# The attention heads' gate as seven half-size products, the residual gate's sums at an earlier place, and a new order of the projections

## The chip, the cores and the metric

The kernel runs on one core of a Trainium2 chip, as one program with one launch. The metric is the device time of that program in microseconds. The engines in the text are PE (TensorE), DVE (VectorE), ACT (ScalarE) and POOL (GpSimd). SP (SyncE) does no arithmetic here: it issues nearly all transfers between the chip's memory and the on-chip buffers, in one queue, in order.

## The reference, cut to what matters

One layer with 1,024 latent tokens (`x`), 256 context tokens and a model width of 1,024. Both token sets are normalised and modulated, then multiplied by one wide input matrix whose output is cut into eleven parts.

```
pl = project(modulate(x, sh_x, sc_x), w_in)       # gq gk gv gg lr dq dk dv dg mg md
pc = project(modulate(ctx, sh_c, sc_c), w_in)
o_gla  = bidir_gla(...)                           # gated linear attention, from gq gk gv and the decay
o_diff = diff_attention(...)                      # from dq dk dv, over context and latent keys
a = merge_heads(rms_norm(o_gla) * gla_gain) * silu(gla_gate)              # gla_gate  = pl[3] (gg)
b = merge_heads(rms_norm(o_diff) * diff_gain * (1 - lam_init)) * silu(diff_gate)   # diff_gate = pl[8] (dg)
y = sigmoid(m_gla) * (a @ w_br_gla) + sigmoid(m_diff) * (b @ w_br_diff)
x = x + g_x * (y @ w_out)                         # g_x: the last third of silu(c) @ w_ada + b_ada
```

`dg` is the part that this change computes in another way: 1,024 tokens by 1,024 columns from an inner width of 1,024. `g_x` is the residual gate.

## The kernel before

Matrix products keep near float32 precision by cutting each operand into a high and a low part, so every product of tiles is three PE instructions (`mm3`, high by high, high by low, low by high). A piece of weight comes by DMA into a `raw` buffer (three of them, 512 KB each), ACT writes the high part and DVE the low part (`split`), both into tiles called `w` (18 of them, so nine pairs).

The order of instructions on PE, ACT, DVE and POOL is not written out. Tasks (Python generators) run under a planner, `Driver`, which keeps its own estimate of every engine's clock and lets the ready task of the best priority write its next instructions. PE then runs what it was given strictly in that order. SP's order is set by another scheduler. Stages in order of time:

1. The modulated inputs `h` are made, then the projections gk, gq and gg (first half of the columns) run on PE. Beside them run the decays (`job_la`, tiles `gs`, `go`, `gt` into `g5`) and `sums`, in which DVE adds and subtracts blocks of `h` (S2, S1, S3, S4), splits them and stores them to `d_s`.
2. `pairs`: the projections gv and dv as seven half-size products (Winograd's form of Strassen's scheme). Rows, columns and inner width are halved. Five tiles of 128 rows (four of latent tokens, one of context) by four inner pieces by seven products by three instructions make 420 PE instructions for one projection; the plain way takes 10 x 8 x 2 x 3 = 480. The left operands S come back from `d_s` through six `g5` buffers (task `loads`). The right operands are sums of weight blocks that DVE makes in place and splits (`pair_weights`). Results are collected in on-chip tiles X, U, U5 with ACT copies and DVE additions (`copy`, `add`, `out`, `direct`).
3. `to_gla` closes the buffers of the pairs and opens those of the GLA; it first waits for the residual gate's store (`ev_gb`). Four GLA heads then run as chains of small PE, ACT, DVE and POOL steps. The other projections (list `late`, plain form) have the lowest priority and fill PE between those steps: dk, second half of gg, second half of dk, first half of dg, first half of dq, one block of mg, second half of dq, second half of dg. At the fourth of them (`n == 3`) `rope_tables(0)` is started, which loads and scales the table that `post_qk` of dq needs.
4. When the last head's results are written, `to_gla` opens the attention's buffers (`ev_b2`); queries `aq`, keys `hk` and values `vv` are loaded, and when the projections are done (`ev_stream`) the attention of the eight heads runs (tiles `s`, `e`, `b`, `mb`). The output product follows.

The residual gate is made by `job_gate`: eight weight pieces of 512 KB pass through the `raw` buffers, DVE multiplies and adds them into `gb` (16 instructions), PE sums over partitions with `ones`, DVE adds the bias, POOL halves it, and one store writes `d_gb`. It is started when the second pair (dv) begins, and its first line waits until all weights of the pairs are loaded (`ev_pl`).

`post_gate` turns a finished tile of gg or dg into its gate: ACT tanh, one DVE instruction, one POOL multiplication by a gain, a store.

Of the kernel before, what the change touches and what calls it, by code (L numbers as in the profile page):

```python
# [20 lines left out]
P = 128  # L21
# [207 lines left out]
class Hybrid:  # L229
# [515 lines left out]
    def job_gate(self):  # L745


        yield self.ev_pl
# [63 lines left out]
    def phase_a(self):  # L812
# [40 lines left out]
        wp = self.pair_weights((C_GV, C_DV), wd.loaded[-1], last)  # L853
# [20 lines left out]
        d.spawn(self.consts_late(), At(105.0), prio=2)  # L874
        d.spawn(self.sums(), prio=3)
# [7 lines left out]

    SUMS = ("s2", "s1", "s3", "s4")

# [32 lines left out]
    def pair_weights(self, cols, ev_load, ev_run):  # L918
# [3 lines left out]
        wp = {(g, n, k): Event() for g in range(2) for n in RIGHT for k in range(4)}  # L922
# [4 lines left out]
        ev_l = {(g, n, kk): Event() for g in range(2) for n, kk, _ in LOADS}  # L927
# [13 lines left out]
        def run():  # L941
            yield ev_run
            for g in range(2):
# [43 lines left out]
    def pairs(self, wp):  # L987
# [3 lines left out]
        def loads():  # L991

            for g in range(2):
# [4 lines left out]
            for g in range(2):  # L998
# [22 lines left out]
        def mms(g, n, k, t, pm, first, last):  # L1021
# [5 lines left out]
            if t == 4:  # L1027
# [6 lines left out]
        for g in range(2):  # L1034
            if g:
                d.spawn(self.job_gate(), prio=2)
# [4 lines left out]
            def out(g, r, c, t, x, tag):  # L1041

                o = self.tok(8 + r if t == 4 else 4 * r + t)
                if g == 0:
                    self.store([(self.d_v[c][o:o + P], x)], (tag, 1))
                    return
# [39 lines left out]
            for t in range(5):  # L1086
# [7 lines left out]
            for n, ev, dst, nxt, tag in (("p6", "x", U, "u", "x2"), ("p5", "u", U5, "u5", "p")):  # L1094
                for k in range(4):
                    for t in range(5):
# [5 lines left out]
            for t in (0, 1, -1, 2, -2, 3, -3, 4, -4, -5):  # L1102
# [9 lines left out]
            for k in range(4):  # L1112
                for t in range(5):
# [6 lines left out]
    def direct(self, g, t, pm, tag):  # L1120

        o = self.tok(8 if t == 4 else t)
        if g == 0:
# [216 lines left out]
    def post_gate(self, dif, c, i, pm):  # L1340
# [6 lines left out]
        self.rel("mm", e)  # L1347
# [1075 lines left out]
```

## Time and profile before

| | us |
|---|---|
| median of 3 runs | 1690.53 |
| lowest and highest | 1687.66, 1690.86 |
| the profiled execution | 1693.12 |
| its span, first to last instruction | 1691.4 |
| PE busy in the span | 1649.2 (98%) |
| DVE, ACT, POOL busy | 1140.7 (67%), 781.4 (46%), 617.6 (37%) |

The rows used stand in a section further down. The page gives totals and the chain of work that ended last; the stage table gives busy time per engine and stretch, the granted clock as a share of full speed, and the share of time and the rate at which the 16 DMA engines moved data; the timeline gives single instructions, with the engine's idle time before them in brackets. PE instructions overlap: the duration of one is longer than the distance from its start to the next one's, so a price per instruction is read from a merged run of many.

### The profile page before, as it was taken

The page shows a single profiled execution, that of the slowest core. Times are in us where ns is not written, and L with a number is a line of the kernel's source. Part 1 is how long each engine was busy: PE and PEld are TensorE (multiplying, and loading weights), DVE is VectorE, ACT ScalarE, POOL GpSimd, SP SyncE. Part 2 cuts the span into 40 slices and gives each one's busy share as a digit, 9 for nine tenths or more (in the row PEclk, how much of TensorE's full clock was granted, in tenths as well). Part 3 has the DMA queues.
Part 4 walks back from the last instruction along what each step waited for, and adds up shares of the span by engine and source line. Part 5 has one row for each costly group of instructions (what it writes and reads, how often), then busy time and mean ns, then how long its engine had stood idle before and what let it go on. Part 6 is the DMA issues. An engine that isn't in the chain of part 4 may idle for free.

```text
span 1691.4 us, 24621 instructions
## 1 busy us (share of the span) xinstructions
PE 1649.2 (98%) x8437; PEld 1366.0 (81%) x8437; DVE 1140.7 (67%) x2027; ACT 781.4 (46%) x1632; POOL 617.6 (37%) x743
## 2 busy tenths in 40 slices
PE   7999999999999999999999999999999899999999
PEld 3788888888888888888887788888887787887887
DVE  4787743466856866775553988777787787526694
ACT  4766522343444445455232666655656555411231
POOL 1500300002554655553342555455665455700000
PEclk9999999999999999999999999999999999999999
DMA  8556847588737466453851444436368451279431
GB/s 306 172 202 235 303 159 266 178 280 284 224 119 222 134 177 197 131 177 108 245 163 53 106 116 122 129 91 162 104 172 251 140 164 60 91 234 340 151 100 75
DMA packets 259950, 293.43 MB, mean 173 GB/s; under 512 B 21961, under 2 KB 182641, under 8 KB 259825
## 3 DMA queue, kind: packets, MB, share of 16 engines
q1 hardware_dynamic: 259824, 291.85, 55.0%
q8 instruction: 67, 1.10, 0.3%
q14 instruction: 59, 0.48, 0.1%
HBM read 194.27 MB, written 97.52 MB: 173 GB/s over the span
## 4 chain that ended last, share of the span: by engine, by line
PE 82%; DVE 7%; DMA 5%; ACT 2%; issue 2%; POOL 2%; SPq 0%; DVEq 0%; ACTq 0%; POOLq 0%
PE mm L335 33%; PE mc L335 10%; PE mb L335 7%; PE s L335 6%; PE b L335 5%; PE go L335 4%; PE b L361 3%; PE tp L335 3%; PE gt L335 3%; DVE sm L197 3%; PE gs L335 3%; PE tp L361 2%; POOL at L197 2%; DVE e L197 1%; ACT e L197 1%
## 5 line engine op out<-in xcount | busy, mean ns | idle before, releaser
L335 PE MATMUL mm<-w,h 128*128 128x512 f32 x1608 | 401.6, 400 | 0.0
L335 PEld LDWEIGHTS mm<-w,h 128*128 128x128 f32 x1608 | 297.4, 188 | 60.1 <-issue 0.5
L197 DVE TENSOR_REDUCE sm<-s 128x1 f32<-128x1024 f32 (+1 forms) x192 | 194.5, 1038 | 23.9 <-PE s L335 22.0
L335 PE MATMUL mb<-h,wt 128*128 128x512 f32 x744 | 205.1, 408 | 2.5 <-ACT ft L197 2.1
L197 ACT ACTIVATE e<-s,sm 128x1280 f32<-128x1280 f32 x128 | 170.1, 1331 | 69.2 <-DVE sm L197 61.5
L197 POOL TENSOR_TENSOR at<-ac,at 128x512 fp32r<-128x512 f32 x128 | 185.1, 1446 | 10.7
L335 PE MATMUL s<-hk,aq 128*128 128x512 f32 (+1 forms) x768 | 180.7, 369 | 4.1 <-issue 1.5
L197 POOL TENSOR_SCALAR at<-ac 128x512 fp32r<-128x512 f32 x128 | 100.7, 787 | 202.2 <-ACT ac L197 182.6
L335 PEld LDWEIGHTS mb<-h,wt 128*128 128x128 f32 x744 | 131.1, 190 | 25.9 <-ACT ft L197 3.6
L335 PEld LDWEIGHTS s<-hk,aq 128*128 128x128 f32 x768 | 124.3, 193 | 24.9 <-ACT e L197 4.9
L335 PE MATMUL mm<-h,w 128*128 128x512 f32 x576 | 142.4, 398 | 1.4 <-DVE h L197 1.0
L335 PE MATMUL mc<-h,wt 128*128 128x512 f32 x600 | 140.8, 392 | 1.4 <-DVE wt L197 0.5
L197 POOL TENSOR_TENSOR sm<-sm,nhalf 128x1 f32<-128x1 f32 (+2 forms) x110 | 113.8, 1035 | 56.4 <-DVE sm L197 49.6
L335 PEld LDWEIGHTS mc<-h,wt 128*128 128x128 f32 x600 | 111.4, 188 | 26.1 <-DMA h<-d_bT 2.4
L335 PE MATMUL b<-at,vv 128*128 128x256 f32 x960 | 131.9, 287 | 0.5 <-POOL at L197 0.4
L335 PEld LDWEIGHTS b<-at,vv 128*128 128x128 f32 x960 | 124.1, 192 | 5.7 <-POOL at L197 1.2
L335 PEld LDWEIGHTS mm<-h,w 128*128 128x128 f32 x576 | 106.1, 188 | 23.6 <-DVE h L197 1.5
L197 ACT ACTIVATE p<-mm 128x512 f32<-128x512 f32 (+1 forms) x111 | 64.1, 587 | 130.0 <-PE mm L335 112.0
L197 ACT ACTIVATE ac<-b 128x512 f32<-128x512 f32 x120 | 71.3, 601 | 89.6 <-PE b L361 84.4
L197 DVE SCALAR_TENSOR_TENSOR e<-e,sm,e 128x1280 f32<-128x1280 f32 x64 | 108.7, 1699 | 0.6
L197 DVE TENSOR_TENSOR w<-raw,w 128x512 fp32r<-128x512 f32 x120 | 88.0, 751 | 29.1 <-ACT w L197 24.2
L361 PE MATMUL b<-ident,e 128*128 128x128 f32 x598 | 93.3, 277 | 14.2 <-DVE b1k L197 4.8
(282 smaller groups left out, 2697.4 us busy)
## 6 DMA issues: line engine op xcount, KB each, us to landing
raw<-in_w_in SPq DMA_DIRECT2D x66, 512.0 KB, 4.7
g<-d_s SPq DMA_DIRECT2D x32, 640.0 KB, 5.3
aq<-d_qT SPq DMA_DIRECT2D x128, 128.0 KB, 3.1
d_dv<-pl SPq DMA_DIRECT2D x40, 256.0 KB, 5.3
d_kT<-pl SPq DMA_DIRECT2D x40, 256.0 KB, 2.9
gv<-d_v SPq DMA_DIRECT2D x40, 256.0 KB, 3.2
hk<-d_kT SPq DMA_DIRECT2D x32, 320.0 KB, 5.2
vv<-d_dv SPq DMA_DIRECT2D x16, 640.0 KB, 5.9
```

The lines of the kernel that those rows point to most:

```text
L197: self.ins = f(out, *args, **kw).ins
L335: self.ins = self.nc.tensor.matmul(out, lhsT, rhs, start=start, stop=stop, skip_group_check=more).ins
L361: self.nc.tensor.transpose(out, src, self.ident[:n, :n])
```

## The change

`dg` leaves the plain projections and becomes the third member of `pairs`, after gv and dv, for the latent tokens only: four tiles of rows in place of five, `nt = 4 if what == "dg" else 5`. Its left operands are the first 512 columns of the stored S. The gate of three of its four blocks is made from the on-chip sums in `out` (tanh, one DVE instruction, one POOL multiplication), that of the last from the accumulator in `direct` by `post_gate`. `job_gate` no longer waits for `ev_pl` and is started at the planner's time 110, beside the projections gq and gg. The list `late` is now dk, dk, second half of gg, dq, dq and, put in at place 5, mg; at `n == 3`, where `rope_tables(0)` is started, stands the first half of dq.

```diff
     def job_gate(self):
-        yield self.ev_pl
...
-        dg = nat(C_DG, (x8, x8), lambda c, i, pm: self.post_gate(1, c, i, pm))
-        late = [dk[0], gg[1], dk[1], dg[0], dq[0], dq[1], dg[1]]
+        late = [dk[0], dk[1], gg[1], dq[0], dq[1]]
         NM = 1
         for m in range(NM):
             late.insert(5, tra(C_MG + m * 512, ...))
...
-        wp = self.pair_weights((C_GV, C_DV), wd.loaded[-1], last)
+        wp = self.pair_weights([c for _, c in self.BY7], wd.loaded[-1], last)
...
+        d.spawn(self.job_gate(), At(110.0), prio=2)
...
+    BY7 = (("gv", C_GV), ("dv", C_DV), ("dg", C_DG))
...
+            for g, (what, _) in enumerate(self.BY7):
+                w = 512 if what == "dg" else 640
...
-                        z = self.t("g5", [P, 2, 640], F32R)
-                        self.dma(z, self.d_s[n, k])
+                        z = self.t("g5", [P, 2, w], F32R)
+                        self.dma(z, self.d_s[n, k][:, :, :w])
...
-        for g in range(2):
-            if g:
-                d.spawn(self.job_gate(), prio=2)
+        for g, (what, _) in enumerate(self.BY7):
+            nt = 4 if what == "dg" else 5
...
+                if self.BY7[g][0] == "dg":
+                    yield from self.acq("p")
+                    th = self.t("p", [P, 512])
+                    yield d.on("ACT", x)
+                    yield On(self.act.activation(th, x, AF.Tanh, scale=0.5), "DVE")
+                    e = self.dve.scalar_tensor_tensor(x, th, 1.0, x, ALU.add, ALU.mult)
+                    self.rel("p", e)
+                    yield e
+                    xv = x.rearrange("p (n w) -> p n w", w=P)
+                    self.pool.tensor_tensor(xv, xv, self.gdif..., ALU.mult)
+                    self.store([(self.d_dg[c][...], x)], (tag, 1), ev=...)
+                    return
...
-            for t in (0, 1, -1, 2, -2, 3, -3, 4, -4, -5):
+            for t in (0, 1, -1, 2, -2, 3, -3, 4, -4, -5) if nt == 5 else (0, 1, -1, 2, -2, 3, -3, -4):
```

In the program's order this shows at three places. The first is PE at the end of dv. Before, the first tile of dk follows, eight inner pieces into one accumulator `mm`; `h` are the pieces of the modulated input.

```order
L335 MATMUL mm_3564<-w_3455,h_73_382 128x512
L335 MATMUL mm_3564<-w_3456,h_73_382 128x512
L335 MATMUL mm_3564<-w_3455,h_74_383 128x512
L335 MATMUL mm_3564<-w_3465,h_131_582 128x512
L335 MATMUL mm_3564<-w_3466,h_131_582 128x512
L335 MATMUL mm_3564<-w_3465,h_132_583 128x512
```

The same place of the changed program, where dg's products begin:

```order
L335 MATMUL mm_3596<-w_3487,h_73_382 128x512
L335 MATMUL mm_3596<-w_3488,h_73_382 128x512
L335 MATMUL mm_3596<-w_3487,h_74_383 128x512
L335 MATMUL gt_3611<-w_3518,h_131_582 128x512
L335 MATMUL gt_3611<-w_3519,h_131_582 128x512
L335 MATMUL gt_3611<-w_3518,h_132_583 128x512
```

After the fourth inner piece the accumulator changes from `mm` to `gt`: two products of half the inner width stand where one of the full width stood. Over the whole program PE has 48 rows fewer, DVE 41 more, ACT 24 more, SP 18 more and POOL as many as before.

The second place is DVE at the start of the projection gg, where the low parts of its seventh and eighth weight pieces are made. Before (`w_1720` and `w_1732` are those two; `g` and `x` belong to `sums` and to the decays):

```order
L197 TENSOR_TENSOR w_1683<-raw_1391,w_1682 128x512
L197 TENSOR_TENSOR g_314_1561<-g_314_1561,x_331_1681 128x640
L197 TENSOR_SCALAR g_336_1698<-gs_1699,col 128x512
L197 TENSOR_SCALAR g_336_1698<-go_1702,col 128x512
L197 TENSOR_SCALAR g_336_1698<-gt_1706,col 128x256
L197 TENSOR_TENSOR w_1720<-raw_1652,w_1719 128x512
L197 TENSOR_TENSOR g_314_1561<-g_314_1561,x_334_1696 128x640
L197 TENSOR_TENSOR w_1732<-raw_1652,w_1731 128x512
```

The same stretch now, where `w_1754` and `w_1762` are the two pieces:

```order
L197 TENSOR_TENSOR w_1698<-raw_1623,w_1697 128x512
L197 TENSOR_TENSOR g_318_1580<-g_318_1580,g_317_1579 128x640
L197 TENSOR_SCALAR gb_1143<-raw_1667,col 128x512
L197 TENSOR_SCALAR g_341_1710<-gs_1711,col 128x512
L197 SCALAR_TENSOR_TENSOR gb_1143<-raw_1667,col,gb_1143 128x512
L197 TENSOR_TENSOR g_317_1579<-g_317_1579,x_339_1708 128x640
L197 TENSOR_SCALAR g_341_1710<-go_1716,col 128x512
L197 TENSOR_SCALAR g_341_1710<-gt_1720,col 128x256
L197 TENSOR_TENSOR w_1754<-raw_1695,w_1753 128x512
L197 TENSOR_TENSOR g_317_1579<-g_317_1579,x_345_1728 128x640
L197 TENSOR_TENSOR w_1762<-raw_1695,w_1761 128x512
```

Two instructions of the residual gate and one more of `sums` now stand between the sixth weight piece and the seventh.

The third place is SP at the end of the GLA. `d_aT` are its last results, `aq` the attention's first queries, `d_qT` the queries of the projection dq, `vv` the attention's values. Before, with plain projections still to come:

```order
L300 DMA d_aT_99<-gpl_8261 128x2x128
L300 DMA aq_8323<-d_qT_86 64x2x256 x2
L300 DMA aq_8326<-d_qT_86 64x2x256 x2
L300 DMA aq_8329<-d_qT_86 64x2x256 x2
L300 DMA aq_8332<-d_qT_86 64x2x256 x2
L300 DMA d_qT_87<-pl_8300 128x4x128
L300 DMA d_qT_87<-pl_8301 128x4x128
L300 DMA vv_8378<-d_dv_82 128x10x128
L300 DMA vv_8380<-d_dv_84 128x10x128
```

The same place of the changed program, where `d_m` are stores of the mg block and `raw` the next weights:

```order
L300 DMA d_aT_99<-gpl_8894 128x2x128
L300 DMA d_m_117<-p_8907 128x512
L300 DMA aq_8936<-d_qT_86 64x2x256 x2
L300 DMA aq_8939<-d_qT_86 64x2x256 x2
L300 DMA aq_8942<-d_qT_86 64x2x256 x2
L300 DMA aq_8945<-d_qT_86 64x2x256 x2
L300 DMA raw_8968<-in_w_in 128x8x128
L300 DMA vv_8979<-d_dv_82 128x10x128
L300 DMA vv_8981<-d_dv_84 128x10x128
L300 DMA vv_8983<-d_dv_82 128x10x128
L300 DMA raw_8999<-in_w_in 128x8x128
L300 DMA d_m_118<-p_9001 128x512
```

One store of the mg block (`d_m`) now stands ahead of the queries, and only two such stores are left behind them: on PE 54 products of mg stand between the GLA's last instruction and the attention's first, where 351 products of dq and dg stood. From the attention's first instruction on, the order on PE (3,161 rows), DVE and ACT is the same in both programs.

## Rows read from the trace of the kernel before

**Rows 1.** The page: busy time and share of each engine, then the last chain.

```profile
PE 1649.2 (98%) x8437; PEld 1366.0 (81%) x8437; DVE 1140.7 (67%) x2027; ACT 781.4 (46%) x1632; POOL 617.6 (37%) x743
...
PE 82%; DVE 7%; DMA 5%; ACT 2%; issue 2%; POOL 2%; SPq 0%; DVEq 0%; ACTq 0%; POOLq 0%
```

**Rows 2.** Busy time by stage, from gq to the attention's start; columns in its first line.

```profile
core 0: us, PE busy (x) PEld busy (x) DVE busy (x) ACT busy (x) POOL busy (x), PEclk, DMA share, GB/s
100.00:160.00 60.00, 60.00 (x313) 51.56 (x312) 45.17 (x67) 42.42 (x61) 0.00 (x0) 1.00 0.59 212
160.00:208.80 48.80, 48.80 (x217) 40.40 (x216) 40.16 (x51) 26.79 (x39) 11.88 (x8) 1.00 0.87 318
208.80:303.60 94.80, 94.80 (x420) 78.51 (x419) 40.34 (x62) 28.48 (x49) 1.40 (x1) 1.00 0.61 217
303.60:398.40 94.80, 93.92 (x412) 77.08 (x412) 53.93 (x84) 34.53 (x60) 0.62 (x1) 1.00 0.71 245
398.40:442.00 43.60, 43.60 (x203) 35.62 (x202) 33.10 (x54) 10.51 (x19) 21.36 (x24) 1.00 0.86 268
442.00:825.50 383.50, 382.06 (x1932) 320.88 (x1931) 256.81 (x508) 185.44 (x525) 199.34 (x331) 1.00 0.56 164
825.50:910.60 85.10, 83.60 (x384) 68.77 (x383) 39.52 (x64) 20.26 (x33) 34.10 (x31) 1.00 0.50 144
```

**Rows 3.** Timeline of PE: start, length, instructions, idle before; first gg, then dv.

```profile
161.85 4.24 PE L335 MATMUL mm<-w,h 128*128 128x512 f32 x18
...
166.50 42.35 PE L335 MATMUL mm<-w,h 128*128 128x512 f32 x186
...
381.08 0.97 PE L335 MATMUL tp<-w,hk 128*128 128x512 f32 x3 [0.88 <-DVE p L197]
```

**Rows 4.** Groups by line: count, then busy us, mean ns, idle before.

```profile
L197 DVE TENSOR_TENSOR w<-l,w 128x512 fp32r<-128x512 f32 x28 | 18.7, 687 | 16.9 <-ACT w L197 16.9
...
L197 DVE SCALAR_TENSOR_TENSOR gb<-raw,col,gb 128x512 f32<-128x512 f32 x14 | 11.4, 814 | 4.9 <-DMA raw<-in_w_ada 4.8
...
L197 ACT ACTIVATE w<-l 128x512 fp32r<-128x512 f32 x28 | 17.0, 626 | 17.3 <-PE go L335 15.6 <-PE mm L335 1.5
...
L197 POOL TENSOR_TENSOR p<-p,gdif 128x512 f32<-128x512 f32 x16 | 22.0, 1379 | 35.8 <-DVE p L197 35.6 <-PE gt L361 0.2
...
L335 PE MATMUL go<-gv,gsc 128*128 128x256 f32 x64 | 19.1, 381 | 0.2 <-DVE gsc L197 0.2
```

**Rows 5.** DMA issues: count, KB each, median us to landing.

```profile
g<-d_s SPq DMA_DIRECT2D x32, 640.0 KB, 5.3
...
raw<-in_w_ada SPq DMA_DIRECT2D x12, 512.0 KB, 6.0
```

**Rows 6.** Timeline of SP and DVE: gg's last weight piece, load and split.

```profile
156.36 0.38 SPq L300 DMA_DIRECT2D raw<-in_w_in  x1
...
165.38 0.68 DVE L197 TENSOR_TENSOR w<-raw,w 128x512 fp32r<-128x512 f32 x1
```

**Rows 7.** Timeline of POOL and DVE beside a gate's multiplication in gg.

```profile
172.69 2.42 POOL L197 TENSOR_TENSOR p<-p,ggla 128x512 f32<-128x512 f32 x1 [86.75 <-DVE p L197]
...
173.88 1.78 DVE L197 TENSOR_TENSOR g<-h,h 128x512 f32<-128x512 f32 x1
...
175.79 0.68 DVE L197 TENSOR_TENSOR g<-h,h 128x512 f32<-128x512 f32 x1
```

**Rows 8.** Timeline of PE and SP from the GLA's last instruction to the attention's first.

```profile
825.17 0.38 PE L361 MATMUL tp<-ident,gp 128*128 128x128 f32 x2
...
827.57 5.05 SPq L300 DMA_DIRECT2D aq<-d_qT  x8
...
910.60 2.56 PE L335 MATMUL s<-hk,aq 128*128 128x512 f32 x12 [1.50 <-issue]
```

More of the change, by code (lines that the diff above doesn't have):

```diff
@@ L921, in pair_weights @@
         RIGHT = ("w11", "w21", "t2", "t1", "t3", "t4", "v22")
-        wp = {(g, n, k): Event() for g in range(2) for n in RIGHT for k in range(4)}
+        wp = {(g, n, k): Event() for g in range(len(cols)) for n in RIGHT for k in range(4)}
         slots = {}
@@ L926, in pair_weights @@
                  ("w22", 1, "x4"), ("w12", 1, "raw"), ("v22", 0, "raw"), ("v22", 1, "l5"))
-        ev_l = {(g, n, kk): Event() for g in range(2) for n, kk, _ in LOADS}
+        ev_l = {(g, n, kk): Event() for g in range(len(cols)) for n, kk, _ in LOADS}
         def load():
@@ L942, in run @@
             yield ev_run
-            for g in range(2):
+            for g in range(len(cols)):
                 def blk(n, k):
@@ L991, in loads @@
         def loads():
-            for g in range(2):
+            for g in range(len(self.BY7)):
                 for n in self.SUMS:
@@ L997, in loads @@
             yield self.ev_la
-            for g in range(2):
+            for g, (what, _) in enumerate(self.BY7):
+                w = 512 if what == "dg" else 640
                 for n in self.SUMS:
@@ L1026, in mms @@
             e = self.mm3(pm, sh, sl, *wp[g, W[n], k].w, first, last, True)
-            if t == 4:
+            if t == nt - 1:
                 self.rel("w", e, 2)
@@ L1032, in mms @@
             return e
-        for g in range(2):
-            if g:
-                d.spawn(self.job_gate(), prio=2)
+        for g, (what, _) in enumerate(self.BY7):
+            nt = 4 if what == "dg" else 5
             A, B, TBt = [None] * 5, [None] * 5, [None] * 5
@@ L1043, in out @@
                 o = self.tok(8 + r if t == 4 else 4 * r + t)
-                if g == 0:
+                if self.BY7[g][0] == "dg":
[7 more added lines that the diff above has]
+                    xv = x.rearrange("p (n w) -> p n w", w=P)
+                    self.pool.tensor_tensor(xv, xv, self.gdif.unsqueeze(1).to_broadcast([P, 4, P]), ALU.mult)
+                    self.store([(self.d_dg[c][(4 * r + t) * P:(4 * r + t + 1) * P], x)], (tag, 1),
+                               ev=self.ev_st["dg", c, 4 * r + t])
+                    return
+                if self.BY7[g][0] == "gv":
                     self.store([(self.d_v[c][o:o + P], x)], (tag, 1))
@@ L1084, in outer @@
                 return e
-            for t in range(5):
+            for t in range(nt):
                 yield from self.acq(TA[t])
@@ L1095, in pairs @@
                 for k in range(4):
-                    for t in range(5):
+                    for t in range(nt):
                         if k == 0:
@@ L1112, in pairs @@
             for k in range(4):
-                for t in range(5):
+                for t in range(nt):
                     if k == 0:
@@ L1122, in direct @@
         o = self.tok(8 if t == 4 else t)
-        if g == 0:
+        if self.BY7[g][0] == "dg":
+            self.d.spawn(self.post_gate(1, 1, t, pm, tag), prio=-1)
+            return
+        if self.BY7[g][0] == "gv":
             yield from self.acq("p")
@@ L1338, in post_qk, with post_gate @@
                    ("pl", 2), ev=self.ev_st["dk" if isk else "dq", c, i])
-    def post_gate(self, dif, c, i, pm):
+    def post_gate(self, dif, c, i, pm, tag="mm"):
         nc = self.nc
@@ L1346, in post_gate @@
         e = self.dve.scalar_tensor_tensor(th, th, 1.0, pm, ALU.add, ALU.mult)
-        self.rel("mm", e)
+        self.rel(tag, e)
         w = P if dif else 256
```

## The prediction, made before the changed kernel was run

> **What bounds the kernel now.** The first view is the page with each engine's busy time: PE is busy 98% of the span, DVE 67%, ACT 46%, POOL 37%, and 82% of the chain that ended last is PE's own [rows 1]. That is an average, so the next view is the table by stage. In every stage from gq to the attention's start PE is full: the pair gv takes 94.80 us and is busy for all of them, dv stops for 0.88 us, the GLA stage stops for 1.44 us of 383.5 (383.5 less 382.06), all at a granted clock of 1.00, the upper level [rows 2]. So here an instruction taken from PE is worth its full length, provided that nothing which PE waits for becomes later. The price is read from the stage that is full and has one kind of instruction: 94.80 us for 420 products, 0.2257 each [rows 2]; a merged run of 186 plain products in gg takes 42.35 us, 0.2277 each [rows 3]. Half-size and plain products cost the same.
>
> After that the groups by line give the prices of the steps beside PE, the DMA issues those of loads, and the timeline the two or three places where the order changes [rows 4 to 8].
>
> The clock of the sum: the profiled execution took 1693.12 us, 2.59 above the median of 1690.53. I work against the profiled one and take 2.59 off at the end.
>
> **The change part by part.**
>
> *dg as seven products.* Plain, it is 384 products; now four tiles by four inner pieces by seven by three, 336. The order of the changed program has those 48 PE rows fewer. 48 x 0.2257 = 10.8 us, all on PE, which is full. Term: −10.8.
>
> What feeds the new stage, 336 x 0.2257 = 75.8 us long: DVE makes 28 low parts, 16 sums of weights, 12 additions and 16 gates; at 0.687 us, the low part's price [rows 4], 72 x 0.687 = 49.5 us, 65% of the stage. gv's stage has 40.34 us in 94.80 and did not stop; dv's has 53.93 us, 57%, and stopped once [rows 2]. ACT makes 28 high parts, 12 copies and 16 tanh at 0.626: 35 us. POOL multiplies 16 gates at 1.379: 22 us [rows 4]. Transfers: 16 S pieces and 10 weight pieces of 512 KB in and 4.2 MB out make some 17.8 MB, 235 GB/s, where gg's stage ran at 318 [rows 2]. An S piece is 512 KB instead of 640 KB but is used up in four tiles instead of five, so the needed rate is dv's. I see no engine that ends late, but DVE has less room than in either older pair. Bounds: nothing, or one S load wholly exposed, 5.3 x 512/640 = 4.2 us [rows 5]. I take +0.5, near the row of dv (one stop of 0.88 at 57%). The gates' stores and the table work are covered by the GLA's 383 us that follow.
>
> *The residual gate, moved out of dv.* dv's one stop, 0.88 us on a DVE result [rows 3], falls in the stretch where DVE also carried most of the gate's 14 multiply-and-adds at 0.814 [rows 4] and was 13.6 us busier than in gv (53.93 less 40.34) [rows 2]. I give it back whole: −0.9.
>
> *The residual gate, moved into gq and gg.* Everything it issues moves: eight loads of 512 KB on SP through the three `raw` buffers that the projections' weights use too, 16 DVE instructions, the sums with `ones` on PE, one POOL step, one store. The stages it joins: gq with DVE 45.17 of 60 us and 212 GB/s, gg with DVE 40.16 of 48.80 us (82%) and 318 GB/s at a DMA share of 0.87 [rows 2]. This is the tightest place of the change. gg's last weight piece is issued at 156.36 and its low part starts on DVE at 165.38, ending at 166.06 [rows 6]. PE reaches the seventh piece at 166.50 [rows 3], so the eighth three products later, 167.18: a lead of 1.1 us. The order puts two instructions of the gate and one more of `sums` in DVE's row ahead of the seventh: at most 0.81 + 0.81 + 0.68 = 2.3 us [rows 4, 7]. So 2.3 − 1.1 = 1.2, say 1.0 us, reaches PE. If a load of the gate also holds DVE, whose multiply-and-adds waited 4.8 us for such loads in dv [rows 4], it is up to 4.9. Queued behind the waiting instruction are then the projection's own low parts, and PE waits for these. The two sums with `ones` stand in PE's row in gq and in gg, behind a DVE result; a wait there holds the whole projection. No row shows that wait at the new place; bounds 0 and 2 us each, and I take 1.0 each, by dv's 0.88 stop on DVE. Term: +3.0, from 0 to 9 (4.9 + 2 x 2).
>
> *Less plain work beside the GLA, in another order.* From the GLA's last instruction to the attention's first, 351 products stood before; now 54, that is 12.2 us. The tail of 85.1 us, in which PE was busy 83.60 [rows 2], thus mostly goes: its work lies in the GLA stage or is gone. The stage has 1,122 filler products in place of 1,104, so its PE time hardly changes, but its fillers are now dk, gg, dq and mg, and dk's and dq's tiles need more DVE steps than dg's. The order gives DVE 573 instructions there instead of 523; at the stage's mean of 256.81/508 = 0.506 us [rows 2] that is 25 us more, 282 us or 73% in place of 67%. PE's stop was 1.44 us; `go`, the product nearest to the chain of a head, waited 0.2 us in all 64 [rows 4]. I take that the stop doubles: +1.5, from 0 to 5.4 (0.506 us on every third of the 32 blocks). The table that dq's finishing needs, formerly loaded under dg's first half, is now loaded under the last dk and gg work; that cover is long enough.
>
> *The attention's start.* Before, the last two dg tiles passed ACT and DVE ahead of the first `s`, which stood idle 1.50 us [rows 8]; now mg's last tiles need ACT alone, and one DVE step of 0.68 goes: −0.6. The risk is on SP: queries were issued from 827.57, 2.4 us after the GLA's last transposes at 825.17 [rows 8], and 83 us lay ahead of them; now 12.2 do. Issue 2.4 us late, eight issues in 5.05 [rows 8] and a landing of 5.3 [rows 5] give 12.8 at most, and one more store stands ahead of them on SP. So it fits barely, or costs up to 5 if a landing is exposed whole.
>
> Sum: −10.8 − 0.9 + 3.0 + 0.5 + 1.5 − 0.6 = −7.3. 1693.1 − 7.3 = 1685.8, and less 2.6: **1683.2 us**. With every unknown cost at nothing (−12.3) it is 1678.2.
>
> **The rivals.**
>
> *D, all of it hidden: 1678.2.* For it: PE stopped 1.44 us in 383 us of GLA. Against it: the 1.1 us of lead at gg, which the order uses up.
>
> *C, the gate at its full price: +9 in place of +3, 1689.2.* For it: gg's stage has the highest DVE share and the highest DMA rate of the stages ahead of the attention, and the gate's loads share buffers and queue with its weights. A POOL gate in gg also holds DVE: the addition `g<-h,h` took 1.78 us beside POOL's `p<-p,ggla` and 0.68 otherwise [rows 7]. Against it: only the seventh and eighth piece of gg show so short a lead, and a late piece delays PE once, not for each instruction behind it.
>
> *B, POOL's gates hold DVE in dg's stage: 1692.0.* The pair of lengths in rows 7, 1.78 and 0.68, is 1.1 us per POOL multiplication. The stage has 16 of them, where gv's and dv's had at most one POOL instruction [rows 2]: 17.6 us more on DVE, 67.1 of 75.8 us (89%). If half of it reaches PE, 8.8 us, the gain is 1.5. Against it: DVE's additions read an accumulator and one buffer, and only the low parts and weight sums read two buffers. The Trainium skill, page "SBUF — State Buffer", section "Who interferes with whom", says that a VectorE instruction with two inputs in SBUF contends with a GpSimd instruction that reads SBUF, and that whichever issues second waits for the whole of the first. By that rule this rival applies to the low parts and weight sums of the stage. The trace agrees at 173.88 us, where the two overlap [rows 7].
>
> *A, slower: the GLA's heads become late: 1697.7.* A mechanism with one place: in each of the 32 blocks (pairs of the 64 `go`) one DVE instruction of dk's or dq's finishing, 0.506 us on the mean, stands ahead of the step that PE's next head product waits for. 32 x 0.506 = 16.2 in place of 1.5 makes the sum +7.4 in place of −7.3. It decides from 8.8/32 = 0.28 us per block on. For it: DVE at 73%. Against it: `go` waited 0.2 us in all, so DVE at 67% left a long lead, and fillers stand between.
>
> *The change does not do what it says.* If dg's products did not fall, sooner sums alone would bring only the 0.9 of dv, as PE is full everywhere. The order shows the 48 rows gone, so this has no chance of its own.
>
> **How the numbers follow.** Forecast (1680 to 1687.5) 60%, D 14%, C 13%, B 7%, A 6%. About 0.2%, 3.4 us, is what a measurement of this kernel tells from no change; so faster means under 1687.1, slower over 1693.9. Faster: 56 of the forecast's 60, D's 14, 4 of C and 1 of B, 75. Slower: A's 6 and 1 of B, 7. Same: the remaining 18. Range: A is left out above with part of B, and half of D below: 1677 to 1692.
>
> **What the changed profile would show.** PE's count 48 lower. After dv a stage of 336 products in some 76 us; a longer one with DVE instructions of 1.7 us beside POOL's `gdif` multiplications is B. At gg's first tile a stop of about 1 us behind a `w` from DVE, and a stop at each `ones` product; many us there is C. GLA stage with PE idle of 2 to 4 us; `go` or the head products waiting on DVE for 16 is A. Between the GLA's last instruction and the first `s` some 12 us and an idle of about 1 us; 5 or more behind a DMA of `aq` or `vv` is the queries' risk. The forecast is wrong if PE's stops outside these four places change, above all in the attention, whose order of instructions is the same in both programs.

## The result, and the profile after

The changed kernel is slower. Its median is 1696.26 us (14 runs, 1692.24 to 1698.73), that of the kernel before in the same comparison 1689.06 us (14 runs); the ratio is 1.0035, with a 95% interval of 1.0027 to 1.0043. The forecast was 1683.2, faster.

The profiled execution after took 1693.18 us, with a span of 1691.4 us, the same span as the profiled execution before; the execution after lies 3.1 us under its kernel's median, the one before 2.6 to 4.1 us over (medians of 3 and of 14 runs). So the two profiles are compared stretch by stretch and not by their spans. That the spans are equal comes from the late attention: between 1300 and 1460 us the mean granted clock was 0.95 before and 0.98 after, which is worth some 5 us, and the order of instructions there is the same. The page of the profile after, its busy time and its last chain, against [rows 1]:

```profile
PE 1643.7 (97%) x8389; PEld 1358.2 (80%) x8389; DVE 1164.2 (69%) x2067; ACT 792.1 (47%) x1656; POOL 618.9 (37%) x743
...
PE 76%; DVE 10%; DMA 5%; issue 3%; ACT 3%; POOL 3%; SPq 0%; DVEq 0%; ACTq 0%; POOLq 0%
```

PE has 48 instructions fewer, and the chain that ended last has 6% of the span less on PE: in its place stand DVE, ACT, POOL and issue.

The stage table, cut at the first product of each stage. Before: gq and gg from 100 us on, gv, dv, everything from dk to the attention's first `s`, and the next 12 us. After: the same, with dg as a stage of its own behind dv. Columns as in [rows 2].

```profile
100.00:205.96 105.96, 105.96 (x516) 89.59 (x515) 82.49 (x114) 68.44 (x98) 10.29 (x6) 1.00 0.71 258
205.96:301.16 95.20, 95.20 (x421) 78.83 (x420) 42.09 (x63) 28.01 (x49) 2.99 (x2) 1.00 0.60 215
301.16:398.40 97.24, 96.36 (x423) 79.13 (x422) 55.02 (x85) 35.77 (x63) 0.62 (x1) 1.00 0.72 249
398.40:910.60 512.20, 509.25 (x2515) 425.26 (x2514) 329.43 (x624) 216.22 (x577) 254.80 (x384) 1.00 0.57 170
910.60:922.70 12.10, 12.09 (x62) 9.95 (x62) 8.07 (x13) 4.41 (x7) 2.22 (x3) 1.00 0.27 89
```

```profile
100.00:212.84 112.84, 109.44 (x522) 90.51 (x522) 93.76 (x133) 69.72 (x98) 13.44 (x8) 1.00 0.80 279
212.84:308.04 95.20, 95.20 (x421) 78.83 (x420) 42.09 (x63) 27.95 (x49) 2.99 (x2) 1.00 0.64 229
308.04:403.73 95.69, 95.47 (x421) 78.57 (x419) 48.82 (x75) 34.99 (x62) 0.00 (x0) 1.00 0.70 249
403.73:483.25 79.52, 78.02 (x336) 62.87 (x337) 50.89 (x72) 32.81 (x59) 17.37 (x13) 1.00 0.64 213
483.25:909.74 426.49, 422.13 (x2130) 354.51 (x2128) 297.19 (x585) 194.90 (x544) 239.04 (x372) 1.00 0.59 170
909.74:928.70 18.96, 14.80 (x62) 11.95 (x62) 8.39 (x13) 4.33 (x8) 0.44 (x1) 0.82 0.61 163
```

| stretch | before | after | difference | forecast |
|---|---|---|---|---|
| gq and gg | 105.96 | 112.84 | +6.9 | +3.0 |
| gv | 95.20 | 95.20 | 0 | 0 |
| dv | 97.24 | 95.69 | −1.6 | −0.9 |
| dg, and dk to the first `s` | 512.20 | 79.52 + 426.49 | −6.2 | −9.4 |
| first 62 products of the attention | 12.10 | 18.96 | +6.9 | 0 |
| sum | | | +6.0 | −7.3 |

(−9.4 is −10.8 + 0.5 + 1.5 − 0.6.) At 100 us PE of the changed kernel is 0.6 us behind already: one and the same product starts at 102.20 us before and at 102.78 after. So 0.6 of the +6.9 in gq and gg was lost ahead of them. From the end of the table the order of instructions is the same in both, and the stretch of the next 540 products is as long in both within 0.2 us. The +6.0 stands against the medians' 7.2.

Three stops of PE that the kernel before did not have make most of it. The timeline at the three places (the DMA line and the ACT line ahead of the last stop are its cause):

```profile
196.87 1.12 PE L335 MATMUL tp<-gb,ones 128*128 128x512 f32 x2 [2.51 <-DVE gb L197]
...
720.07 0.44 PE L361 MATMUL gt<-ident,ge 128*128 128x128 f32 x2 [3.37 <-POOL ge L197]
...
904.98 5.04 SPq L300 DMA_DIRECT2D vv<-d_dv  x3
908.41 1.28 ACT L197 ACTIVATE p<-mm 128x512 f32<-128x512 f32 x2 [7.71 <-PE mm L335]
909.74 2.60 PE L335 MATMUL s<-hk,aq 128*128 128x512 f32 x12 [0.69 <-ACT p L197]
...
912.35 2.16 SPq L300 DMA_DIRECT2D d_m<-p  x2
...
919.12 1.33 ACT L197 ACTIVATE e<-s,sm 128x1280 f32<-128x1280 f32 x1 [9.44 <-DMA d_m<-p]
...
920.59 2.08 PE L335 MATMUL s<-hk,aq 128*128 128x512 f32 x4 [4.16 <-ACT e L197]
```

The first is at the second of the residual gate's two sums with `ones` (two PE instructions each), in gg: 2.51 us on DVE. The second is the last GLA head: 3.37 us on `ge`, a tile of the head's preparation that POOL finishes. The third lies behind the first `s`: ACT's first exponential `e` waits 9.44 us, the last part of it for a store of mg, because the attention's buffer for `e` lies where the projections' buffers `p` lay. mg's last two tiles are ready at 909.7; SP issues their stores at 912.35, behind the values and weights, and the second has landed at about 919.

The table of stretches by granted clock adds the rest (PE alone; the columns behind its busy time are the granted clock, the DMA share and GB/s). After:

```profile
180.00:200.00 20.00, 17.49 (x76) 1.00 0.83 283
200.00:220.00 20.00, 20.00 (x90) 1.00 0.88 317
700.00:720.00 20.00, 16.70 (x85) 1.00 0.93 293
720.00:740.00 20.00, 19.93 (x89) 0.91 0.39 112
900.00:920.00 20.00, 15.75 (x70) 0.98 0.90 243
920.00:940.00 20.00, 19.28 (x87) 0.85 0.17 56
```

Behind the second and the third stop the granted clock is at its lower level (1.2 instead of 2.4 GHz) for a while: 0.91 over 20 us is 1.8 us of work lost. At the third, part of the low clock falls into the stop itself; the 62 products take 14.80 us of busy time in place of 12.09, so 2.7 us of work are lost. Before, the granted clock was 1.00 from gq to the attention's start [rows 2]. So of the +6.0 us 4.5 are clock, lost behind stops; the stops and smaller waits themselves have eaten the 10.8 us that the products gave.

### The profile page after: what moved, and what is told of

It is laid out like the page before. It is cut to its first block, busy times and chain, and to the rows that moved or that the text cites. A ratio compares the mean times of both kernels' runs of the same rounds, so it can differ in the third digit from the quotient of the medians.

```text
span 1691.4 us, 24649 instructions
## 1 busy us (share of the span) xinstructions
PE 1643.7 (97%) x8389; PEld 1358.2 (80%) x8389; DVE 1164.2 (69%) x2067; ACT 792.1 (47%) x1656; POOL 618.9 (37%) x743
## 4 chain that ended last, share of the span: by engine, by line
PE 76%; DVE 10%; DMA 5%; issue 3%; ACT 3%; POOL 3%; SPq 0%; DVEq 0%; ACTq 0%; POOLq 0%
PE mm L335 26%; PE mc L335 10%; PE mb L335 7%; PE s L335 6%; PE b L335 5%; PE tp L335 5%; PE go L335 4%; PE gt L335 4%; PE b L361 3%; PE gs L335 3%; DVE sm L197 3%; DVE g L197 2%; PE tp L361 2%; POOL at L197 2%; DVE e L197 1%
## 5 line engine op out<-in xcount | busy, mean ns | idle before, releaser
L335 PE MATMUL mm<-w,h 128*128 128x512 f32 x1260 | 326.4, 404 | 0.6 <-DVE w L197 0.4
L335 PEld LDWEIGHTS mm<-w,h 128*128 128x128 f32 x1260 | 231.7, 188 | 47.1 <-DVE w L197 0.8
L197 ACT ACTIVATE w<-raw 128x512 fp32r<-128x512 f32 x120 | 72.6, 628 | 70.7 <-DVE raw L197 22.7
L197 POOL TENSOR_TENSOR p<-p,gdif 128x512 f32<-128x512 f32 x12 | 16.2, 1357 | 242.6 <-DVE p L197 215.2
```

Source lines behind the costliest of these rows:

```text
L197: self.ins = f(out, *args, **kw).ins
L335: self.ins = self.nc.tensor.matmul(out, lhsT, rhs, start=start, stop=stop, skip_group_check=more).ins
```

## The experiments

The theory after the two traces: the seven products are worth what they should be, and three separate stops, two of them with clock lost behind them, take it back: the gate beside gg, the last GLA head, and `e` waiting for mg's stores. Its rivals are named with each run. Ratios are to the kernel before, run beside each.

**The gate alone, early.** The kernel before with this edit:

```diff
-        yield self.ev_pl
...
-            if g:
-                d.spawn(self.job_gate(), prio=2)
...
+        d.spawn(self.job_gate(), At(110.0), prio=2)
```

> The kernel before with one edit: the residual gate starts at the planner's time 110, beside gq and gg, without waiting for the pairs' weights; dg stays plain and the projections keep their order. Theory 1 (the gate itself holds PE at the new place): PE stops of 5 to 6.5 us more in gq and gg, of which 2 to 3 us at the second product with ones; about 1 us of stops gone in dv and dk; the time 3 to 6 us above the kernel before (1692 to 1695). Rival (in the changed kernel the stops in gq and gg come from the reordering as a whole, the gate alone is hidden): stops in gq and gg under 1.5 us, the time within 1.5 us of the kernel before.

Measured: 1700.14 us, ratio 1.0066 (1.0048 to 1.0084), 11.7 us above. The stop in gg is there as in the changed kernel, at the same product and of the same length:

```profile
197.61 2.08 PE L335 MATMUL tp<-gb,ones 128*128 128x512 f32 x2 [2.51 <-DVE gb L197]
```

The cost of the gate at this place is the gate's own, as theory 1 says. The time, though, rose by twice what was expected. In the GLA's stage PE waits 3.8 us in three stops on POOL's `p` and 2.4 us on DVE's `gsb`, which the kernel before did not, and the granted clock falls behind the stop in gg (0.93 and 0.98 over 180 to 220 us) and behind one of those in the GLA (0.91 over 740 to 760 us). All waits of PE together are some 8 us more than before, the clock is worth some 3, so the 11.7 us are found. The planner orders the GLA's stage anew once the gate has gone from dv; that this order makes the stops there is likely, but no run isolates it.

**The gate in gv.** The changed kernel with `At(205.0)` in place of `At(110.0)`.

> The changed kernel with one edit: the residual gate starts at the planner's time 205 in place of 110, so that its products with ones stand in gv; all else is the same. Theory 1 (the gate costs what gq and gg lost): PE stops in gq and gg fall from 6.3 to under 1 us, gv gains under 1.5 us, the time falls by 4 to 6 us against the changed kernel, to about 1691, level with the kernel before within 3 us. Rival (the gate's eight loads and 16 steps hurt wherever they stand, as the raw buffers are shared): gv stops for 4 us or more and the time stays within 2 us of the changed kernel.

Measured: 1702.33 us, ratio 1.0079 (1.0064 to 1.0095): slower by 6 to 7 us than the changed kernel. The rival is right. DVE waits about 4 us for each of three pieces and PE 12.88 us for the sum:

```profile
240.23 1.54 DVE L197 SCALAR_TENSOR_TENSOR gb<-raw,col,gb 128x512 f32<-128x512 f32 x2 [3.90 <-DMA raw<-in_w_ada]
...
253.17 2.08 PE L335 MATMUL tp<-gb,ones 128*128 128x512 f32 x2 [12.88 <-DVE gb L197]
```

In gv the gate's pieces share the three `raw` buffers with the pair's weights, and a product with `ones` that PE's row holds too early stops everything behind it. The loss is smaller than this stop because two others are gone: PE has no stop over 0.8 us in gq and gg, and none behind the first `s`. There mg's last stores are issued at 926.82 us, and `e` starts at 928.26 without waiting for them. So in this run its buffer does not lie on theirs: the projections have five buffers `p` and use them in turn.

**mg ahead of the last half of dq.** The changed kernel with `late.insert(4, ...)` in place of 5.

> The changed kernel with one edit: the mg block stands before the second half of dq, not after it, so the last stores ahead of the attention are queries of its second half and not mg's. Theory 1 (the attention's first exponentials waited 4 us for mg's last stores, which stood on SP behind the values' loads): the first exponential no longer waits for a store of mg, the PE stop of 4.3 us behind the first s is under 1 us, the time falls by 3.5 to 6 us against the changed kernel. Rival (the values' and weights' loads themselves are the wait, since only 12 us of plain work were left to cover them): the wait stays at 3 us or more, behind another transfer, and the time stays within 2 us.

Measured: 1698.65 us, ratio 1.0058 (1.0046 to 1.0070), no gain, but 2 to 4 us slower than the changed kernel. No store of mg is waited for any more, but the end of dq is a longer chain than the end of mg, through ACT, DVE and POOL and back to PE's transposes, and it stands bare, with stops of 5.19, 2.42 and 1.41 us, the first of them:

```profile
913.56 1.11 PE L361 MATMUL tp<-ident,p 128*128 128x128 f32 x4 [5.19 <-POOL p L197]
```

This is not the rival as written, since no load takes the wait over; what is confirmed is that anything at the end of the projections is exposed there.

**The gate late.** The changed kernel with the gate started at the third pair and waiting for `ev_pl`, as in the kernel before.

> The changed kernel with the residual gate at its old place in the sequence: started at the third pair, dg, and waiting for the pairs' weights. The order of its program has no plain work left between the GLA's last instruction and the attention's first, since the GLA's buffers open only when the gate is stored. Theory 1 adds up: 6 us of stops in gq and gg go, but the change from GLA to attention is bare, so the queries' issue and landing (some 6 us) and the stores stand open there and the GLA's stage runs out of other products: slower than the changed kernel by 2 to 15 us. Rival (the early gate brought nothing but its cost): faster than the changed kernel by 4 to 6 us.

Measured: 1698.08 us, ratio 1.0059 (1.0044 to 1.0073), some 2 to 4 us above the changed kernel, at the lower end of what theory 1 expected. The three stops of the changed kernel are not there. In their place PE waits 2.67 us in dg and 1.2 to 1.4 us three times near 770 us, and the GLA's last results come at 914.1 us in place of 896.8. The attention's first product waits for the first queries, which can only be loaded once the GLA's buffers are closed:

```profile
919.28 2.05 PE L335 MATMUL s<-hk,aq 128*128 128x512 f32 x4 [5.51 <-DMA aq<-d_qT]
```

The early gate lets the GLA end early enough, so that the queries' loads are covered. With the gate started only at the third pair they are not.

**e's buffers elsewhere.** The changed kernel with two lines where the attention's buffers are opened; they lay out at4 and ac first, and the order of instructions stays.

```diff
             self.open("psW", "psB", "sbB")
+            self.t("at4", [P, 4, 2, P], F32R)
+            self.t("ac", [P, 4, P])
```

> The changed kernel with one edit: when the attention's buffers are opened, those of at4 and ac are laid out first, so that the first exponentials e no longer lie where the projections' buffers p lay; the order of instructions is the same. Theory 1 (the first e waited for the last stores of mg because it overwrites their buffer): the 9.4 us wait of ACT for a store of mg is gone, the PE stop of 4.3 us behind the first s falls under 1 us, the time falls by 3 to 5 us against the changed kernel (1691 to 1693). Rival (the loads of queries, values and weights into the bare 12 us are the limit): another transfer or POOL's first at takes the wait over within 10 us of it, the time falls by less than 1.5 us.

Measured: 1689.25 us, ratio 0.9996 (0.9985 to 1.0007): the loss of the whole change is gone. The same two places as above:

```profile
913.69 2.60 PE L335 MATMUL s<-hk,aq 128*128 128x512 f32 x12 [0.69 <-ACT p L197]
...
918.09 1.33 ACT L197 ACTIVATE e<-s,sm 128x1280 f32<-128x1280 f32 x1 [4.46 <-DVE sm L197]
```

`e` now waits for its own input from DVE, no stop of PE follows, and the granted clock behind it stays at 1.00 (the row 920 to 940 us):

```profile
920.00:940.00 20.00, 19.86 (x102) 1.00 0.38 122
```

It starts 4.4 us behind the first `s`, where it started 9.4 us behind it in the changed kernel: 5.0 of the 9.44 us were the store's. From 1.0035 to 0.9996 is 0.0039 of 1689, 6.6 us; the stop itself was 4.2 and the work lost to the lower clock behind it 2.7. The loads and the values were no limit: the rival falls.

**The gate through other buffers.** The changed kernel with the gate at 260, in gv and dv, and its pieces in `g5` buffers.

```diff
-                yield from self.acq("raw")
-                raw = self.t("raw", [P, 2, 512])
+                yield from self.acq("g5")
+                raw = self.t("g5", [P, 2, 640])[:, :, :512]
...
-        d.spawn(self.job_gate(), At(110.0), prio=2)
+        d.spawn(self.job_gate(), At(260.0), prio=2)
```

> The changed kernel with the residual gate at the planner's time 260, in gv and dv, its weight pieces passing through g5 buffers, not raw. Theory 1 with what the gate in gv showed (13 us at one product with ones: the pieces stood between the pair's weights in the three raw buffers): no stop over 2 us in gv or dv, the stops in gq and gg under 0.5 us, the time 3 to 5 us below the changed kernel (1691 to 1693). Rival (DVE cannot take the 16 steps beside a pair without holding PE, whatever the buffer): stops of 4 us or more in gv and dv, the time not below the changed kernel's by 1.5 us.

Measured: 1695.31 us, ratio 1.0036 (1.0022 to 1.0050), the same as the changed kernel. The 13 us are gone, which fits the shared buffers, though the start was moved too. The stop behind the first `s` is still there (3.94 us). And now the third accumulation of dg waits for a buffer that dv's last results still hold:

```profile
407.75 0.69 DVE L197 TENSOR_TENSOR p<-gt,p 128x512 f32<-128x512 f32 x1 [1.32 <-PE gt L335]
...
409.74 1.28 DVE L197 TENSOR_TENSOR pl<-mm,pl 128x512 fp32r<-128x512 f32 x2
...
410.48 2.93 PE L335 MATMUL mm<-w,h 128*128 128x512 f32 x6 [2.84 <-DVE pl L197]
```

The split that frees the buffer (`pl<-mm`) stands in DVE's row behind dg's first addition (`p<-gt`), for which DVE waits 1.32 us on PE. In the changed kernel one of the two splits runs ahead of that addition, at 407.90 against 409.50 us, and PE doesn't stop there. The residual gate's multiply-and-adds had ended at 386.8. So the time is as the rival says, but its reason is not shown: there is no stop of 4 us in gv and dv (none over 1 us), and what holds PE is the planner's new order at the start of dg.

**Both edits.** The last two together.

> The changed kernel with both edits, the gate through g5 in gv and dv and e's buffers away from p's. If the two costs are separate they add: 7 to 9 us below the changed kernel, 1687 to 1690, level with the kernel before or up to 2 us faster; the seven products' 10.8 us then still lose some 4 us to the GLA's stop and other small stops. Rival (what is saved early is lost again at the attention, as the queries' and values' loads come earlier by as much): no more than 5 us below the changed kernel.

Measured: 1688.72 us, ratio 1.0003 (0.9992 to 1.0013), 0.0032 below the changed kernel, 5.4 us. That is no more than `e` alone gave; moving the gate this way gave nothing, as in the run before it.

**The products with ones later.** The changed kernel with the planner's time of the two products put 10 us later; the gate's loads and DVE steps stay.

```diff
-            yield self.d.whenpe(gb)
+            yield AtPE(max(self.d.now, self.d.whenpe(gb)) + 10.0)
```

> The changed kernel with one edit: the two products with ones are put 10 us later in the planner's time, the gate's loads and DVE steps stay beside gq and gg. Theory 1a (PE stopped because the products with ones stood too early in its row): the stop of 2.7 us goes, gg's stops fall from 4.3 to about 1.5 us, the time falls by 2 to 3 us. Theory 1b (the low parts of the weights come late behind the gate's DVE steps): the stop of 2.7 us turns into as much waiting for w at gg's or gv's next pieces, the time stays within 1 us.

Measured: 1689.45 us, ratio 0.9999 (0.9988 to 1.0009), 6.1 us below the changed kernel. PE in the stretch with the stop (after: 17.49 busy of 20):

```profile
180.00:200.00 20.00, 19.62 (x87) 1.00 0.85 285
```

Theory 1a holds: the stop is gone (2.1 us more busy time in the row) and PE's longest wait left in gq and gg is 0.5 us. The gain is larger than this trace shows; but the profiled execution was the slowest of the ten (1695.25; the others 1685.47 to 1693.80). Part of the rest is the clock behind the stop, seen in the next run. What makes up the remaining 1 to 2 us stays open.

**The changed kernel again,** beside the next three.

> The changed kernel as it is, beside the next three on the same chip. Both theories: 5 to 8 us slower than the kernel before. Theory 1 says besides that the granted clock falls to its lower level for some microseconds behind the stop at 716 us and the one behind the first s, as in its first profile; a rival (the clock falls at random places) puts it elsewhere.

Measured: 1694.61 us (1688.82 to 1701.19), ratio 1.0032 (1.0016 to 1.0048). The three stops are the same to 0.1 us, but this time the clock fell behind the first and the third, and not behind the second:

```profile
180.00:200.00 20.00, 17.49 (x70) 0.94 0.78 282
200.00:220.00 20.00, 20.00 (x88) 0.98 0.82 297
700.00:720.00 20.00, 17.96 (x91) 1.00 0.95 283
720.00:740.00 20.00, 18.67 (x93) 1.00 0.43 125
920.00:940.00 20.00, 19.65 (x93) 0.91 0.21 68
```

Theory 1 is half right: the clock falls behind these stops and at no other new place, but behind any one of them only in some executions. (Elsewhere it is lower at 40 to 60 us and in the attention between 1340 and 1420 us, as in the profiles without the change.) That fits the spread of the kernel's runs in part: the mean granted clock is 0.998 in the fastest (1688.82), but the slowest (1701.19) has 0.992 and another of 1696.40 has 0.991.

**The control: the kernel before with e's buffers elsewhere** (the edit of the fifth experiment).

> The kernel before with the one edit of e5 (at4 and ac laid out ahead of e). Theory 1 (e over p costs only where the last stores come with no plain work ahead of them): its first e waited for DVE by then, not for a store, so the time stays within 2 us of the kernel before. Rival (the new layout is faster by itself, whatever the change): 3 us or more faster than the kernel before.

Measured: 1689.72 us, ratio 1.0005 (0.9997 to 1.0014). The layout by itself is worth nothing; in the kernel before nothing waited for it: its first `e` waits 5.26 us for DVE's `sm`, and 5.19 us with the edit.

**Two cures.** The changed kernel with e's buffers elsewhere and the products with `ones` 10 us later.

> The changed kernel with the edits of e5 and e8 (e's buffers away from p's, the products with ones 10 us later). Theory 1: the stop of 2.7 us in gg and the one of 4.3 us behind the first s are gone together with the clock lost behind them; 9 to 12 us below the changed kernel, 1684 to 1687, 2 to 5 us below the kernel before. Rival (the two cures save the same time, as the later of them swallows the earlier): no better than e5 alone, 1688 to 1690.

Measured: 1681.70 us (1679.53 to 1684.07), ratio 0.9955 (0.9943 to 0.9967): 7.6 us faster than the kernel before, some 13 faster than the changed one. The two cures add up (0.0039 and 0.0036 singly, 0.0077 together against the changed kernel beside it), and the rival falls. Its stage table, first gq and gg, then from dg on (gv and dv take 95.20 and 95.65 us):

```profile
100.00:209.26 109.26, 108.73 (x521) 90.45 (x520) 93.92 (x131) 68.73 (x98) 13.07 (x8) 1.00 0.79 277
...
400.11:479.16 79.05, 77.75 (x337) 62.88 (x337) 51.12 (x72) 32.84 (x59) 17.38 (x13) 1.00 0.64 213
479.16:903.08 423.92, 420.71 (x2129) 353.31 (x2127) 297.24 (x585) 195.17 (x544) 240.53 (x372) 1.00 0.59 171
903.08:915.20 12.12, 12.11 (x60) 9.94 (x61) 8.11 (x13) 4.37 (x7) 0.35 (x1) 1.00 0.92 246
```

The attention's start takes 12.12 us, as before the change (12.10), and PE is busy 98% of the span again (1638.8 us). The mean granted clock of its runs is 0.9966; that of the kernel before beside it was 0.9969, that of the changed kernel 0.9941.

**Three cures.** As the last, and the last GLA head's scans 6 us later for the planner.

```diff
-            yield self.d.when(lab)
+            yield At(self.d.when(lab) + (h == 3) * 6.0)
             self.dve.memset(lab[:, :, 0:1], 0.0)
```

> As the run with two cures, and the last GLA head's scans are put 6 us later in the planner's time, so that more plain products stand ahead of its first transposes. Theory 1 (the stop of 3.5 us at 716 us is that head's late preparation, and the lower clock behind it costs about 1.8 us more): stop and lower clock at 716 us are gone, 3 to 6 us below the run with two cures. Rival (the head's chain ends the GLA, so a later start of it only moves the wait to its end and to the attention's start): within 1.5 us of the run with two cures, with a new stop of 3 us or more at the end of the GLA or behind the first s.

Measured: 1680.92 us, ratio 0.9953 (0.9939 to 0.9966), the same as with two. PE around the head's start, with two cures and then with three:

```profile
700.00:720.00 20.00, 17.94 (x91) 1.00 0.81 256
```

```profile
700.00:720.00 20.00, 19.93 (x103) 1.00 0.86 268
```

The stop is gone, 2.0 us of busy time more in its stretch; 0.9 us of it is lost again toward the GLA's end, where PE is busy 68.40 us between 840 and 910 us instead of 69.31. The rival is nearer than theory 1: with two cures the stop was only 2.06 us long with no clock lost behind it, and about half of that comes back.

## Why the prediction was wrong

The direction was wrong. From −7.3 to +6.0 are 13.3 us, and in the table the attention's start holds 6.9 of them, gq and gg 3.9, dg with the stage behind it 3.2, while dv came out 0.7 better. The step that failed is the attention's start; the others had the mechanism and missed the size.

*dg as seven products, −10.8: right, but its feeding, +0.5, was too small.* The 48 instructions are gone. The stage has its 336 products (the row from 403.73 us) and is 79.52 us long, 3.7 more than the 75.8 of the sum, against a term of +0.5. PE idles 1.50 of the 3.7 us; the rest is busy time beyond 0.2257 us a product. The largest of PE's waits in that stretch (total, number, longest):

```profile
PE mm L335 <- ACT w L197: 0.6, 2, 0.4
PE mm L335 <- DVE w L197: 0.5, 2, 0.2
PE tp L335 <- DVE p L197: 0.3, 1, 0.3
```

They are small, on high and low parts and on additions; the row of dv was not a good neighbour. DVE is busy 64% here (50.89 of 79.52) and 57% in dv; that this is the reason is not shown. Rival B's blocking is there, but seldom. Four of the DVE instructions in this stage took 1.78 us beside one of POOL's multiplications and 0.68 otherwise, 4.4 us together, the first of them:

```profile
422.67 1.62 POOL L197 TENSOR_TENSOR p<-p,gdif 128x512 f32<-128x512 f32 x1 [4.21 <-DVE p L197]
423.06 1.78 DVE L197 TENSOR_TENSOR l<-l,raw 128x512 f32<-128x512 f32 x1
```

Only one of PE's waits, 0.30 us on an addition of DVE's at 469.50, comes close behind one of the four, so B is not what cost the 3.7 us. (The prediction's text calls +1.5 under B a gain; the sum −7.3 + 8.8 is a loss of 1.5. Rival A's +7.4 gives 1697.9 and not 1697.7.) The same blocking shows in gg: a multiply-and-add of the gate took 1.42 us beside POOL's multiplication and 0.74 at 196.08.

```profile
192.27 2.60 POOL L197 TENSOR_TENSOR p<-p,ggla 128x512 f32<-128x512 f32 x1 [3.70 <-DVE p L197]
...
194.00 1.42 DVE L197 SCALAR_TENSOR_TENSOR gb<-raw,col,gb 128x512 f32<-128x512 f32 x1 [0.27 <-DMA raw<-in_w_ada]
...
196.08 0.74 DVE L197 SCALAR_TENSOR_TENSOR gb<-raw,col,gb 128x512 f32<-128x512 f32 x1
```

It is the rule of the Trainium skill, page "SBUF — State Buffer", section "Who interferes with whom", again: two inputs in SBUF against a GpSimd instruction that reads SBUF. The trace agrees here. The blocking in gg lengthened the stop at the `ones` product by at most the 0.68 us between the last two rows.

*The gate, +3.0 − 0.9: right mechanism, one wait too small.* The table has +6.9 − 1.6. The place was named, the second sum with `ones` in gg behind a DVE result, but priced at 1.0 us by dv's stop of 0.88; it took 2.51. The first sum, in gq, priced at 1.0, did not wait. The parts of the weights, priced at 1.0, took 0.4 on ACT and 0.4 on DVE. Together PE idles 3.4 us there against the +3.0. The rest of the +6.9 is no wait: 0.6 us was lost ahead of 100 us, and the products with `ones` themselves, two pairs of about 0.9 us by the starts around them, moved here out of dv and out of the stage behind it; the sum had them at neither place. Rival C's +9 was a price for waits, and these were 3.4.

*The GLA, +1.5: right in size, wrong in form.* PE idles 3.7 us in the stage behind dg, without the 0.69 at the first `s`, where it idled 1.45 from dk on before (2.95 less 1.50): +2.2. That is one long stop of 3.37 us on `ge` (2.06 in the run with two cures), not a little on each block; `go` has no row among them, so rival A is not what happened. What the step left out is that one long stop also costs clock, 1.8 us in the profiled execution.

*The attention's start, −0.6: this step failed.* The prediction named SP and the bare 12.2 us, and weighed up to 5 us for late queries. The queries came in time: the first `s` waited 0.69 us. What came late were mg's own last stores, one step further on: SP's row shows them behind the values and weights (the third place in the section on the change), and the buffers of `e` lie on those of `p`. A store was counted as the end of a step and not as something that a later buffer waits for. Together with the lower clock it took 6.9 us: 4.16 of stop and 2.7 of work at the lower clock.

*What no step had.* A stop of PE was priced at its own length. Here a stop of 2.5 to 4.2 us costs up to 2.7 us more, because the granted clock behind it can fall. The mean granted clock of the changed kernel's runs in the control, 0.9941, stands 0.0028 below the 0.9969 of the kernel before beside it: 4.7 us of 1690. The prediction said that the forecast would be wrong if stops outside its four places changed, above all in the attention. That sign came: the third stop lies in the attention, behind its first `s`, one step past the last of the four places. The other two lie inside them.

The sum −7.3 is about what the run with two cures measures (−7.6). In the order of the table its stages differ from before by +3.3, 0, −1.6, −9.2 and 0.0 us, against a forecast of +3.0, 0, −0.9, −9.4 and 0. Part of that is luck. In the −9.2 the stage of dg alone is 79.05 us, 2.7 more than forecast, and the stretch from there to the first `s` is shorter by nearly as much. So the run bears out the terms for work and not the judgement of the waits.

## What to carry to other kernels

When work is moved ahead of a stage that used to be followed by cover, list what that cover hid to the last store: a store is over only when it has landed and its buffer may be written again, and the next stage's first tile may lie on that buffer. Where one engine is full, price each new wait by what the order lets run behind it, and count a stop of some microseconds on TensorE with the clock that may be lost after it. An instruction of a side task that stands in the row of the full engine should come late there: here 10 us of slack on the products with `ones` were worth 6 us.

## What the runs showed of the hardware

The granted clock fell to its lower level behind some stops of PE inside otherwise full stretches, and not every time: behind the same stop of 2.51 us it was 1.00 in one profile of the changed kernel and 0.94 in the next, behind the one of 3.37 us 0.91 and then 1.00. The length alone does not decide: behind the stop of 2.06 us of the run with two cures the clock stayed at 1.00, and behind one of 1.93 us at 734 us in the run with the gate in gv it was 0.91 over 720 to 740 us. One such fall cost 1.6 to 2.7 us of work. The changed kernel's runs spread over 12 us (1688.82 to 1701.19, eight runs beside the control), those of the kernel with two cures over 5 (five runs); that the clock makes this difference is likely and not shown.

A VectorE instruction with two inputs in SBUF took 1.78 us where it overlapped a multiplication on POOL and 0.68 us otherwise, in dg's stage four times.
